# Modulation, scaling and first projections tile by tile at the start of a two-layer mixer backbone

## The chip, the cores and the metric

The kernel runs on one core of a Trainium2 chip. The metric is the device time of one execution in microseconds (us), the median over several runs.

## What is computed

A backbone of two layers over 512 tokens (256 of context and 256 latent) with 2048 features. Each layer normalises its input, shifts and scales it by a modulation vector that is computed from `c` (or from `c_ctx` for context tokens), projects it, sends the projections through four token mixers and merges their outputs. What the change touches is the beginning of the first layer:

```python
shift, scale, gate = jnp.split(jax.nn.silu(c) @ w_mod + b_mod, 3, axis=-1)
sh_c, sc_c, gt_c = jnp.split(jax.nn.silu(c_ctx) @ w_mod + b_mod, 3, axis=-1)
h = _rms(x, norm_g) * (1.0 + scale[:, None]) + shift[:, None]
hc = _rms(xc, norm_g) * (1.0 + sc_c) + sh_c
p = h @ w_in
pc = hc @ w_in
```

## The kernel before

The 2048 features lie in 16 feature tiles of 128 partitions, each with all 512 tokens along the free dimension. The sixteen tiles `x` are loaded, squared and summed (`sumsq`), and `rms_rows` makes one row of 512 scale factors of the sums, `rsb`: a matmul with a column of ones, a reciprocal square root on VectorE (`rq_y`), four transposes on TensorE (L305) and a copy on ScalarE (L525).

The modulation: `s32` holds silu of `c` and of `c_ctx`, a column pair per feature tile. `mod_unit` (L477) loads four pieces of `w_mod` of 128 x 512 (tag `mr`, 16 buffers, L487) and multiplies each with a pair of columns (L493). The four matmuls write to four groups of 32 rows of one bank, so that they can run beside each other. Eight units over two chunks of 512 columns (`shift` and `scale` of four feature tiles) accumulate in one bank. After the last unit ScalarE copies the bank to `ms` (L497), four matmuls with a selecting matrix (`sel`, L506) add up the row groups and turn the result, and VectorE adds the bias into `mod` (L509).

`build_h` (L528) makes of a tile `x` the modulated `h`: VectorE multiplies by `rsb`, ScalarE applies scale and shift for each half of the tokens, then rounds to the high part `Ra` (L542), and VectorE takes the low part `Rb`. `weights` (L370) loads a piece of `w_in` (`wr`, five buffers), ScalarE rounds it to `wh` (L375) and VectorE makes the rest `wl`. `mm3` (L379) multiplies with three matmuls: `wh` with `Ra`, `wh` with `Rb`, `wl` with `Ra`. `proj_part` (L385) does so for one name (a tile of 128 outputs) and one group of four feature tiles.

`run` (L1515) goes over the four groups `g` of four feature tiles. For each it builds `h` and then goes over eleven names: six that accumulate in banks of their own over all groups (`names`), and five whose parts are added up in memory (`more`). Beside the names of group `g` run the eight modulation units of group `g + 1`. Ahead of all stand the eight units of group 0:

```python
for _ in mods(0):
    pass
for g in range(4):
    s.build_h(xs, rsb, 4 * g, 4 * g + 4)
    md, done = mods(g + 1) if g < 3 else iter(()), 0
    for i, _ in enumerate(feats(g)):
        while done * nf < (i + 1) * 8:
            next(md, None)
            done += 1
```

All these loads are issued by SyncE in order. A scheduler below the program decides, within the dependencies, in which order each engine's instructions stand; the engines then take them in that order.

Of the kernel before, what the change touches and what calls it, by code (L numbers as in the profile page):

```python
# [13 lines left out]
ALU = mybir.AluOpType  # L14
# [32 lines left out]
_FI = {n: i for i, n in enumerate(_FN)}  # L47
# [6 lines left out]
_PO, _o = {}, 0  # L54
# [51 lines left out]
def pack(inp):  # L106
    f = lambda n: np.asarray(inp[n], dtype=np.float32)
    d = {}
    d["xT"] = np.ascontiguousarray(np.concatenate([f("ctx")[0], f("x")[0]], 0).T.reshape(KT, 128, T))
    d["cc"] = np.ascontiguousarray(np.stack([f("c")[0], f("c_ctx")], 1).reshape(KT, 128, 2).transpose(1, 0, 2))  # L110
    d["wmod"] = np.ascontiguousarray(f("w_mod").reshape(L, 16, 128, 12, 512).transpose(0, 3, 1, 2, 4))
    wi = f("w_in")
    win = np.zeros((L, _AB, 4, 128, 4, 128), np.float32)
    for n, i in _FI.items():
# [13 lines left out]
    par = np.zeros((L, 128, NPAR), np.float32)  # L128
# [20 lines left out]
    for n, a in (("al", f("d_alog")), ("dt", f("d_dtb"))):  # L149
        o, _ = _PO[n]  # L150
# [17 lines left out]
def wide(ap, n):  # L168

    return ap.rearrange("p (m o) -> p m o", o=1).to_broadcast([ap.shape[0], ap.shape[1], n])  # L170
# [17 lines left out]
class Kern:  # L188
# [193 lines left out]
        s.mm(ps, w[0], x[1], False, False)  # L382
        s.mm(ps, w[1], x[0], False, last)

    def proj_part(s, ps, l, name, t0, qt, alone=False):  # L385
        hi, lo = s.weights(s.i["win"][l, _FI[name], qt], [128, 4, 128])
        for k in range(4):
            kk = qt * 4 + k
            s.mm3(ps, (hi[:, k, :], lo[:, k, :]), (s.Hh[kk][:, t0:], s.Hl[kk][:, t0:]),
                  kk == 0 or alone and k == 0, kk == 15 or alone and k == 3)  # L390

    def proj_park(s, ps, l, name, t0):
# [84 lines left out]
    def mod_unit(s, l, chunks, u, pools, acc=False, bank=None):  # L477


        nc = s.nc  # L480
        i, nch = u // 4, len(chunks)
        first, last = u == 0, u == 4 * nch - 1
        raws = []
        for g in range(4):
            pool, tag = pools[g % len(pools)]
            raw = s.tl(pool, [128, 512], tag)
            nc.sync.dma_start(raw, s.i["wmod"][l, chunks[i], u % 4 * 4 + g])  # L487
            raws.append(raw)
        if first or not acc:
            s.mps = (bank or s.big)()  # L490
        ps = s.mps
        for g in range(4):
            s.mm(ps[32 * g:32 * g + 32, :], s.s32[:, u % 4 * 4 + g, 6 - 2 * i:38 - 2 * i], raws[g],  # L493
                 not acc or first, not acc or last)
        if last if acc else first:
            s.ms = s.tl(s.rp, [128, 512], "ms")
            nc.scalar.copy(s.ms, ps)  # L497
        elif not acc:
            s.tt(s.ms, s.ms, ps, ALU.add)
        if last:  # L500
            par, mod = s.lp[l]
            bo = _PO["bm"][0]
            w = 2 * nch
            p2 = (bank or s.big)()
            for f in range(4):
                s.mm(p2[:, w * f:w * f + w], s.ms[:, f * 128:(f + 1) * 128], s.c("sel", 0, w))  # L506
            pv = p2[:, 0:4 * w].rearrange("p (f i c) -> p i f c", f=4, c=2)
            for i, n in enumerate(chunks):
                s.tt(mod[:, n * 4:n * 4 + 4, :], pv[:, i], wide(par[:, bo + n * 4:bo + n * 4 + 4], 2), ALU.add)  # L509


    def sumsq(s, acc, x, first):
# [1002 lines left out]
    def run(s):  # L1515
        tc, nc = s.tc, s.nc
        with ExitStack() as ctx:
# [5 lines left out]
            with tc.tile_pool(name="x0", bufs=1) as xp:  # L1523
                acc = s.tl(xp, [128, T], "sqa")
                xs = []
# [5 lines left out]
                rsb = s.rms_rows(acc, xp)  # L1531
# [7 lines left out]
                def mods(g):  # L1539
                    for u in range(8):  # L1540
                        s.mod_unit(0, (g, 4 + g), u, [(xp, "mr")], True)
                        yield

                def feats(g):
                    for ps, name in zip(banks, names):
                        s.proj_part(ps, 0, name, 0, g)
                        if g == 3:
                            s.proj_park(ps, 0, name, 0)
                        yield
                    for name in more:  # L1550
                        ps = s.big()
                        s.proj_part(ps, 0, name, 0, g, True)
                        if g == 0:
                            part[name] = s.tl(xp, [128, T], "q" + name)
                            nc.scalar.copy(part[name], ps)
                        else:
                            s.tt(part[name], part[name], ps, ALU.add)
                        if g == 3:
                            nc.gpsimd.dma_start(s.pd[0][name], part[name])
                        yield  # L1560

                nf = len(names) + len(more)
                for _ in mods(0):
                    pass
                for g in range(4):
                    s.build_h(xs, rsb, 4 * g, 4 * g + 4)
                    md, done = mods(g + 1) if g < 3 else iter(()), 0
                    for i, _ in enumerate(feats(g)):
                        while done * nf < (i + 1) * 8:
                            next(md, None)  # L1570
                            done += 1
                s.done.update((0, name) for name in names + more)
                s.filling = False
            for l in range(L):
# [4 lines left out]
                with tc.tile_pool(name=f"xs{l}", bufs=1) as xp:  # L1579
                    xn, sqa = s.out_proj(xp)  # L1580
                    rsb = s.rms_rows(sqa, xp)
# [41 lines left out]
```

## Time and profile before

| what | us |
|---|---|
| median of 3 runs | 2807.53 |
| the runs | 2801.76, 2807.53, 2811.86 |
| the profiled execution's own time | 2812.09 |
| its span, first to last instruction | 2810.3 |
| mean granted TensorE clock | 0.976 |

The rows below come from the one profiled execution; times in them count from the start of its span. PE is TensorE's matmul, PEld its weight load, DVE VectorE, ACT ScalarE, SPq the instructions of SyncE that issue loads. A matmul of 32-bit floats without rounding has two records; x8 is four such matmuls. A name like `big<-mr,s` gives the written tile and those read; `big`, `mx`, `sc` and `acc` are PSUM banks.

### The profile page before, as it was taken

What the parts mean: (1) busy time and instruction counts of PE and PEld (TensorE: products, weight loads), DVE (VectorE), ACT (ScalarE), POOL (GpSimd) and SP (SyncE); (2) the same over time, 40 slices, a digit from 0 to 9 for tenths busy, and PEclk for the clock granted to TensorE, in tenths of its full rate; (3) what the DMA queues carried; (4) which work ended last, traced back from release to release, by engine and by line L of the source; (5) the groups of instructions that cost most, each with busy time, mean ns of one, the idle gap of its engine ahead of it and who ended that gap; (6) DMA issues with size and microseconds to landing.
All of it is one profiled execution on the core that took longest, in us unless ns stands there. A gap on an engine that the chain in (4) does not pass through costs nothing. (4 is left out here: it accounts for less than half of the span.)

```text
span 2810.3 us, 52526 instructions
## 1 busy us (share of the span) xinstructions
PE 2667.1 (95%) x19438; PEld 2035.5 (72%) x19438; DVE 1834.1 (65%) x5127; ACT 1277.1 (45%) x2737; POOL 180.0 (6%) x436
## 2 busy tenths in 40 slices
PE   7998999999999998999999999999999999999897
PEld 3666666677787777677787756776777877867897
DVE  4337776775486777866553354867866688678775
ACT  3334433443355555654442244444443356445553
POOL 0000000000000101000000000010100010100000
PEclk9999999999999998999999999999989999999999
DMA  9754243323432323325447886322323543423465
GB/s 340 266 188 139 78 134 107 121 87 97 122 123 68 101 92 99 97 61 161 151 115 261 272 279 204 112 80 63 110 67 94 161 139 100 128 88 93 144 190 160
DMA packets 210049, 385.80 MB, mean 137 GB/s; under 512 B 24640, under 2 KB 37824, under 8 KB 209792
## 3 DMA queue, kind: packets, MB, share of 16 engines
q1 hardware_dynamic: 199872, 351.23, 40.1%
q0 software_dynamic: 9920, 31.20, 3.0%
q8 instruction: 153, 2.51, 0.4%
q14 instruction: 104, 0.85, 0.1%
HBM read 346.95 MB, written 35.39 MB: 136 GB/s over the span
## 5 line engine op out<-in xcount | busy, mean ns | idle before, releaser
L283 PE MATMUL big<-Rb,wh 128*128 128x512 f32 (+1 forms) x3280 | 1097.3, 363 | 14.9 <-ACT Rb L1347 6.2
L375 ACT CAST wh<-wr 128x512 fp32r<-128x512 f32 x712 | 439.0, 620 | 801.3 <-PE big L283 572.3
L283 PE MATMUL big<-Ra,wh 128*128 128x512 f32 (+1 forms) x2128 | 771.9, 363 | 7.6 <-DVE po L315 3.4
L312 DVE TENSOR_TENSOR wl<-wr,wh 128x512 fp32r<-128x512 f32 x712 | 487.0, 687 | 335.3 <-ACT wh L375 299.6
L283 PEld LDWEIGHTS big<-Rb,wh 128*128 128x128 f32 x3280 | 610.8, 191 | 124.1 <-ACT raw L309 10.9
L283 PE MATMUL big<-Ra,wl 128*128 128x512 f32 (+1 forms) x1616 | 592.9, 367 | 5.2 <-DVE wl L312 5.1
L283 PEld LDWEIGHTS big<-Ra,wh 128*128 128x128 f32 x2128 | 405.9, 191 | 83.9 <-issue 9.9
L283 PE MATMUL big<-Rb,wl 128*128 128x512 f32 (+1 forms) x1088 | 379.7, 349 | 0.9 <-DVE wl L312 0.9
L283 PEld LDWEIGHTS big<-Ra,wl 128*128 128x128 f32 x1616 | 308.6, 191 | 51.1 <-DVE wl L312 6.5
L283 PEld LDWEIGHTS big<-Rb,wl 128*128 128x128 f32 x1088 | 207.4, 191 | 25.2 <-DVE wl L312 1.1
L312 DVE TENSOR_TENSOR iX<-iX,it 128x60 f32<-128x60 f32 (+24 forms) x744 | 182.7, 246 | 17.8
L312 DVE TENSOR_TENSOR it<-iB,iX 128x60 f32<-128x60 f32 (+24 forms) x744 | 173.7, 233 | 17.3
L315 DVE SCALAR_TENSOR_TENSOR po<-po,big 128x512 f32<-128x512 f32 (+1 forms) x128 | 70.4, 550 | 76.4 <-PE big L283 73.6
L283 PE MATMUL big<-Rb,wr 128*128 128x256 f32 (+1 forms) x448 | 112.4, 427 | 3.8 <-DVE Ra L315 2.4
L309 ACT ACTIVATE po<-big,gb 128x512 f32<-128x512 f32 (+1 forms) x128 | 74.0, 578 | 68.5 <-PE big L283 52.7
L283 PE MATMUL big<-mr,s 128*32 128x512 f32 x384 | 86.3, 619 | 17.5 <-DVE sqa L312 17.5
L283 PEld LDWEIGHTS big<-Rb,wr 128*128 128x128 f32 (+1 forms) x448 | 72.5, 183 | 25.0 <-issue 9.0
L315 DVE SCALAR_TENSOR_TENSOR cz<-raw,par,cz 128x508 f32<-128x508 f32 (+3 forms) x96 | 67.2, 700 | 6.0 <-ACT cz L309 5.4
L309 ACT ACTIVATE sw<-S,wc 128x64 f32<-128x64 f32 x96 | 33.4, 348 | 82.7 <-DVE S L315 75.3
L632 DVE TENSOR_REDUCE mx<-mx 128x1 f32<-128x512 f32 (+1 forms) x96 | 57.0, 598 | 20.8 <-PE mx L283 19.9
L283 PE MATMUL mx<-pT,avt 128*64 128x128 f32 x640 | 62.1, 292 | 1.5 <-ACT pT L658 1.3
L305 PE MATMUL mx<-cst,pt 128*128 128x128 f32 x320 | 52.9, 286 | 7.8 <-ACT pt L309 7.5
(373 smaller groups left out, 3760.2 us busy)
## 6 DMA issues: line engine op xcount, KB each, us to landing
wr<-in_win SPq DMA_DIRECT2D x440, 256.0 KB, 2.8
mr<-in_wmod SPq DMA_DIRECT2D x320, 256.0 KB, 4.9
wr<-in_wbr SPq DMA_DIRECT2D x128, 256.0 KB, 2.7
wr<-in_wout SPq DMA_DIRECT2D x128, 256.0 KB, 3.1
wr<-in_wmod SPq DMA_DIRECT2D x64, 256.0 KB, 3.8
wr<-in_gup SPq DMA_DIRECT2D x64, 256.0 KB, 2.7
x<-in_xT SPq DMA_DIRECT2D x16, 256.0 KB, 5.4
po<-y SPq DMA_DIRECT2D x16, 256.0 KB, 3.1
```

What stands on the lines that cost most here:

```text
L283: s.nc.tensor.matmul(o, l, r, start=start, stop=stop)
L305: s.nc.tensor.transpose(o, i, s.c("id"))
L309: s.nc.scalar.activation(o, i, f, bias=bias, scale=scale, **k)
L312: s.nc.vector.tensor_tensor(o, a, b, op)
L315: s.nc.vector.scalar_tensor_tensor(o, a, sc, b, op0, op1)
L375: s.nc.scalar.copy(hi, raw)
L632: nc.vector.tensor_reduce(mx[:, hc], ps[:, 0:nk], AX.X, ALU.max)
```

## The change

The first group of feature tiles is no longer modulated by eight units of whole chunks, but tile by tile. `mod_fine(k)` loads `shift` and `scale` of tile `k` alone, out of a copy of `w_mod` laid out for it (`wmf`, eight loads of 128 x 512), multiplies with 32 matmuls of 128 columns and one `sel` matmul, and adds the bias. Then tile `k` is built and the six `names` are projected for this tile alone, with weight pieces of 128 x 128. After the fourth tile the five `more` names follow with whole pieces, and beside these the eight units of group 1. Groups 1 to 3 are as before.

```diff
+    wm = f("w_mod")[0, :, 0:4096].reshape(4, 4, 128, 2, 16, 128)[:, :, :, :, 0:4]
+    d["wmf"] = np.ascontiguousarray(wm.transpose(4, 3, 0, 2, 1, 5))
...
-    def proj_part(s, ps, l, name, t0, qt, alone=False):
-        hi, lo = s.weights(s.i["win"][l, _FI[name], qt], [128, 4, 128])
-        for k in range(4):
+    def proj_part(s, ps, l, name, t0, qt, alone=False, ks=(0, 4)):
+        hi, lo = s.weights(s.i["win"][l, _FI[name], qt][:, ks[0]:ks[1], :], [128, ks[1] - ks[0], 128])
+        for k in range(*ks):
             kk = qt * 4 + k
-            s.mm3(ps, (hi[:, k, :], lo[:, k, :]), (s.Hh[kk][:, t0:], s.Hl[kk][:, t0:]),
+            s.mm3(ps, (hi[:, k - ks[0], :], lo[:, k - ks[0], :]), (s.Hh[kk][:, t0:], s.Hl[kk][:, t0:]),
                   kk == 0 or alone and k == 0, kk == 15 or alone and k == 3)
...
+    def mod_fine(s, k, pool):
+
+        ps, nc = s.big(), s.nc
+        for i in range(2):
+            raws = []
+            for g in range(4):
+                raw = s.tl(pool, [128, 512], "mr")
+                nc.sync.dma_start(raw, s.i["wmf"][k, i, g].rearrange("p a b -> p (a b)"))
+                raws.append(raw)
+            for c in range(4):
+                for g in range(4):
+                    s.mm(ps[32 * g:32 * g + 32, 0:128], s.s32[:, 4 * g + c, 6 - 2 * i:38 - 2 * i],
+                         raws[g][:, c * 128:c * 128 + 128], i == c == 0, i == 1 and c == 3)
+        ms = s.tl(s.rp, [128, 512], "ms")[:, 0:128]
+        nc.scalar.copy(ms, ps[:, 0:128])
+        p2 = s.big()
+        s.mm(p2[:, 0:4], ms, s.c("sel", 0, 4))
+        par, mod = s.lp[0]
+        bo = _PO["bm"][0]
+        for i in range(2):
+            s.tt(mod[:, 16 * i + k, :], p2[:, 2 * i:2 * i + 2], par[:, bo + 16 * i + k:bo + 16 * i + k + 1].to_broadcast([128, 2]),
+                 ALU.add)
...
-                def feats(g):
-                    for ps, name in zip(banks, names):
-                        s.proj_part(ps, 0, name, 0, g)
+                def feats(g, ks=(0, 4), only=None):
+                    for ps, name in zip(banks, names) if only != "more" else ():
+                        s.proj_part(ps, 0, name, 0, g, ks=ks)
...
-                for _ in mods(0):
-                    pass
-                for g in range(4):
-                    s.build_h(xs, rsb, 4 * g, 4 * g + 4)
-                    md, done = mods(g + 1) if g < 3 else iter(()), 0
-                    for i, _ in enumerate(feats(g)):
-                        while done * nf < (i + 1) * 8:
+                def beside(feats, n, md):
+                    done = 0
+                    for i, _ in enumerate(feats):
+                        while done * n < (i + 1) * 8:
                             next(md, None)
                             done += 1
+
+
+                s.mod_fine(0, xp)
+                for k in range(4):
+                    s.build_h(xs, rsb, k, k + 1)
+                    if k < 3:
+                        s.mod_fine(k + 1, xp)
+                    for _ in feats(0, (k, k + 1), "main"):
+                        pass
+                beside(feats(0, only="more"), len(more), mods(1))
+                for g in range(1, 4):
+                    s.build_h(xs, rsb, 4 * g, 4 * g + 4)
+                    beside(feats(g), len(names) + len(more), mods(g + 1) if g < 3 else iter(()))
```

SyncE's loads behind those for the first tile. In the kernel before, the last loads of group 0's modulation (`mr`) and the first of the weights (`wr`), with the semaphores that each waits for (DMAHW of earlier loads, PE and DVE of those engines):

```order
L487 DMA mr_467<-in_wmod 128x512 [waits DMAHW2_49,PE_49]
L487 DMA mr_469<-in_wmod 128x512 [waits DMAHW3_49,PE_49]
L372 DMA wr_518<-in_win 128x512 [waits DMAHW4_49]
L487 DMA mr_536<-in_wmod 128x512 [waits DMAHW5_49,PE_49]
L487 DMA mr_538<-in_wmod 128x512 [waits DMAHW6_49,PE_49]
```

With the change, from the last load for tile 1, over those for tile 2, to the weight piece of tile 1 that comes last:

```order
L521 DMA mr_474<-in_wmf 128x512 [waits DMAHW3_49]
L375 DMA wr_498<-in_win 128x128 [waits DMAHW4_49]
...
L375 DMA wr_534<-in_win 128x128 [waits DMAHW0_49]
L521 DMA mr_562<-in_wmf 128x512 [waits DMAHW1_49,PE_49]
L375 DMA wr_543<-in_win 128x128 [waits DMAHW4_49,DMAHW2_49,DVE_49]
L521 DMA mr_564<-in_wmf 128x512 [waits DMAHW3_49,PE_49]
...
L521 DMA mr_592<-in_wmf 128x512 [waits DMAHW1_49,PE_49]
L375 DMA wr_616<-in_win 128x128 [waits DMAHW2_49,DVE_49]
...
L521 DMA mr_680<-in_wmf 128x512 [waits DMAHW7_49,PE_49]
L375 DMA wr_661<-in_win 128x128 [waits DMAHW2_49,DMAHW0_49,DVE_49]
```

The sixth weight piece of each tile (`wr_543`, `wr_661`) now waits for VectorE, and seven loads of the tile after next stand behind it.

TensorE between two tiles, with the change: the last short matmuls of tile 2's modulation stand ahead of tile 1's first projection (`Ra_557`):

```order
L286 MATMUL acc_377<-Ra_439,wh_545 128x512
L286 MATMUL acc_377<-Rb_440,wh_545 128x512
L286 MATMUL big_561<-mr_564,s_4_254 32x128
L286 MATMUL acc_377<-Ra_439,wl_546 128x512
L286 MATMUL big_561<-mr_566,s_4_254 32x128
...
L286 MATMUL big_561<-mr_592,s_4_254 32x128
L286 MATMUL mx_372<-Ra_557,wh_618 128x512
L286 MATMUL mx_372<-Rb_558,wh_618 128x512
L286 MATMUL big_612<-cst_87,ms_610 128x4
```

In the kernel before there are no short matmuls; group 0's modulation is done there before the first projection.

TensorE at the end of the first group. Before, the `sel` matmuls (`big_809`) are followed by the last feature's twelve projections, and then by group 1's first (`Ra_842`):

```order
L283 MATMUL big_774<-Ra_514,wl_778 128x512
L283 MATMUL big_809<-cst_87,ms_807 128x4 x4
L283 MATMUL big_816<-Ra_490,wh_819 128x512
...
L283 MATMUL big_816<-Ra_514,wl_820 128x512
L283 MATMUL mx_372<-Ra_842,wh_872 128x512
```

With the change, the last unit's matmuls and `sel` (`big_1055`) come behind the last feature, and group 1's first projection (`Ra_1067`) behind four unit matmuls:

```order
L286 MATMUL big_1020<-Ra_793,wl_1024 128x512
L286 MATMUL big_880<-mr_1043,s_4_254 32x512
L286 MATMUL big_880<-mr_1045,s_4_254 32x512
L286 MATMUL big_880<-mr_1047,s_4_254 32x512
L286 MATMUL big_1055<-cst_87,ms_1053 128x4 x4
L286 MATMUL big_1121<-mr_1113,s_4_254 32x512
...
L286 MATMUL big_1121<-mr_1119,s_4_254 32x512
L286 MATMUL mx_372<-Ra_1067,wh_1097 128x512
```

VectorE ahead of the first freed weight buffer, with the change (`wl_501` is the split of `wr_498`, whose buffer `wr_543` takes):

```order
L318 SCALAR_TENSOR_TENSOR gs_433<-mod_259,par_257 128x2
L315 TENSOR_TENSOR Rb_440<-raw_435,Ra_439 128x512
L315 TENSOR_TENSOR raw_1079<-x_21_295,rsb_370 128x512
L315 TENSOR_TENSOR wl_501<-wr_498,wh_500 128x128
```

Two whole-tile operations stand between `gs` and that split.

## Rows read from the trace of the kernel before

**Rows 1.** The page's first part, busy us (share of the span) and instructions.
```profile
PE 2667.1 (95%) x19438; PEld 2035.5 (72%) x19438; DVE 1834.1 (65%) x5127; ACT 1277.1 (45%) x2737; POOL 180.0 (6%) x436
```

**Rows 2.** Busy time by stretch: length, engines, granted clock, DMA share, GB/s.
```profile
0.00:44.00 44.00, 23.75 (x91) 7.18 (x91) 18.40 (x43) 15.50 (x26) 0.21 (x4) 1.00 1.00 357
44.00:90.00 46.00, 45.58 (x198) 27.20 (x199) 14.32 (x24) 16.26 (x30) 0.00 (x0) 0.96 0.87 305
90.00:135.00 45.00, 45.00 (x207) 26.65 (x205) 16.22 (x29) 14.64 (x27) 0.00 (x0) 1.00 0.77 262
```

**Rows 3.** The timeline's weight loads 28 to 39 us, first and last of 16 (start, us).
```profile
28.26 0.14 PEld L283 LDWEIGHTS big<-mr,s 128*32 128x32 f32 x2 [0.54 <-DMA mr<-in_wmod]
...
38.43 0.14 PEld L283 LDWEIGHTS big<-mr,s 128*32 128x32 f32 x2 [0.55 <-DMA mr<-in_wmod]
```

**Rows 4.** The timeline from the row statistics to the first projection.
```profile
23.91 0.16 DVE L315 SCALAR_TENSOR_TENSOR rq_y<-rq_t,rq_y 128x4 f32<-128x4 f32 x1
25.17 0.65 PE L305 MATMUL mx<-cst,rq_y 128*128 128x128 f32 x4
25.86 0.58 ACT L525 COPY rsb<-mx 128x512 f32<-128x512 f32 x1 [8.44 <-PE mx L305]
...
38.43 1.04 PE L283 MATMUL big<-mr,s 128*32 128x512 f32 x2
39.51 0.58 ACT L497 COPY ms<-big 128x512 f32<-128x512 f32 x1 [13.07 <-PE big L283]
...
43.90 0.69 DVE L312 TENSOR_TENSOR Rb<-raw,Ra 128x512 fp32r<-128x512 f32 x1 [1.61 <-ACT Ra L542]
43.92 0.50 PE L283 MATMUL mx<-Ra,wh 128*128 128x512 f32 x1 [1.64 <-ACT Ra L542]
```

**Rows 5.** TensorE's timeline: the first unit matmul, then projections around a whole unit.
```profile
17.51 1.89 PE L283 MATMUL big<-mr,s 128*32 128x512 f32 x2 [17.51 <-DVE sqa L312]
...
62.51 0.39 PE L283 MATMUL mx<-Ra,wh 128*128 128x512 f32 x1
...
65.00 0.39 PE L283 MATMUL mx<-Ra,wl 128*128 128x512 f32 x1
65.32 1.06 PE L283 MATMUL big<-mr,s 128*32 128x512 f32 x8
66.32 0.50 PE L283 MATMUL acc<-Ra,wh 128*128 128x512 f32 x1
66.66 0.39 PE L283 MATMUL acc<-Rb,wh 128*128 128x512 f32 x1
```

**Rows 6.** Small operations: TensorE's timeline, then groups by line with mean ns.
```profile
622.72 0.28 PE L283 MATMUL sc<-vt,tok 64*64 64x64 f32 x4
622.84 0.28 PE L283 MATMUL acc<-AT,vt 64*64 64x64 f32 x4
...
L309 ACT ACTIVATE vn<-sc 128x128 f32<-128x128 f32 x24 | 6.5, 272 | 4.2 <-PE sc L283 4.2
L312 DVE TENSOR_TENSOR mx<-mx,cm 128x128 f32<-128x128 f32 x32 | 9.5, 297 | 16.9 <-PE mx L283 16.7
```

**Rows 7.** Issues of `mr` loads to 60 us: min, median, max ns; us to landing.
```profile
L487 SPq DMA_DIRECT2D mr<-in_wmod x57: 327/328/385, 12.0 to 59.7; - x57
...
DMA to landing us min/median/max: 3.0/5.4/6.9
```

**Rows 8.** TensorE's timeline at the end of the first group.
```profile
85.79 0.95 PE L283 MATMUL big<-cst,ms 128*128 128x4 f32 x8
...
90.00 0.39 PE L283 MATMUL mx<-Ra,wh 128*128 128x512 f32 x1
```

**Rows 9.** Busy time by stretch, as in rows 2, around two falls of the clock.
```profile
45.80:49.20 3.40, 3.40 (x7) 1.01 (x6) 3.25 (x6) 3.13 (x7) 0.00 (x0) 0.52 1.05 383
219.60:221.70 2.10, 0.14 (x2) 0.02 (x1) 2.04 (x5) 1.98 (x4) 0.00 (x0) 1.00 0.00 0
222.90:226.80 3.90, 3.90 (x14) 1.38 (x12) 2.68 (x9) 0.60 (x1) 0.10 (x1) 0.56 0.00 0
```

More of the change, by code (lines that the diff above doesn't have):

```diff
@@ L1549, in feats @@
                         yield
-                    for name in more:
+                    for name in more if only != "main" else ():
                         ps = s.big()
@@ L1560, in feats @@
                         yield
-                nf = len(names) + len(more)
-                for _ in mods(0):
-                    pass
-                for g in range(4):
-                    s.build_h(xs, rsb, 4 * g, 4 * g + 4)
-                    md, done = mods(g + 1) if g < 3 else iter(()), 0
-                    for i, _ in enumerate(feats(g)):
-                        while done * nf < (i + 1) * 8:
+                def beside(feats, n, md):
+                    done = 0
+                    for i, _ in enumerate(feats):
+                        while done * n < (i + 1) * 8:
                             next(md, None)
                             done += 1
+                s.mod_fine(0, xp)
[9 more added lines that the diff above has]
+                    beside(feats(g), len(names) + len(more), mods(g + 1) if g < 3 else iter(()))
                 s.done.update((0, name) for name in names + more)
```

## The prediction

> **What bounds the kernel now.** I read the page's busy shares first: TensorE (PE) is busy for 95% of the span, no other engine for more than 65% [rows 1]. So a gain must come from PE's idle stretches, or from work taken off PE. Then the table by stage, with bounds at the first projection matmul of each group of four feature tiles: 0 to 44 us is the only stretch in which PE is far from full (23.75 us of 44), and the first two groups after it take 46 and 45 us with PE full [rows 2]; so do the other two. After 179 us the order of the instructions is the same in both kernels, so what is won or lost by then is carried to the end. The question is only when each group's first projection starts.
>
> Why does PE wait until 43.92 us? In the waits of its weight loads, PE stands behind the 32 loads of modulation weights (`mr`): from 28.26 to 38.43 us 16 weight-load rows follow each other, each ended by a landing, so one 256 KB load lands every 10.17/15 = 0.68 us [rows 3], with the DMA engines full (share 1.00, [rows 2]). Then comes a chain: `ms` on ScalarE, four `sel` matmuls, the adds into `mod`, `gs`, two activations, the cast to `Ra`, first projection: 39.46 (38.43 + 1.04) to 43.92, 4.5 us [rows 4].
>
> **The change part by part.** The sum is made against the profiled execution, 2812.09 us with a span of 2810.3, which is 0.16% above the median of 2807.53; I carry the difference over.
>
> *Earlier start.* Tile 0 now needs 8 loads, not 32, so the data would be there 24 x 0.68 = 16 us earlier, at about 22 us. Something else is then late: the row statistics. Their last `rq_y` ends at 24.07, their transposes ran only at 25.17, queued on PE behind full-length `mr` matmuls, and `rsb` is ready at 26.44 [rows 4]. With short ones ahead the transposes start about 1 us earlier, at 24.1. Behind them stand 27 or so of tile 0's 32 short matmuls. PE starts slowly: a matmul of 512 columns took 1.89 us at 17.51, where four beside each other took 1.06 at 65.32 [rows 5]. In that ratio a short round of four, 0.25 us later on (below), takes 0.45 here: seven rounds, 3.2 us, to 27.9. The chain of 4.5 us shrinks: `ms` is 128 wide (0.3 for 0.58), one `sel` matmul (0.3) stands for four (0.95, [rows 8]): 3.5 us. First projection at about 31.5, **12.4 us earlier**. Bounds: 30.0 if the short matmuls already run at the higher level, 32.5 if the chain keeps all but 0.1 us of its 4.5.
>
> *Short matmuls.* Per tile there are 32 matmuls of 128 columns, in rounds of four beside each other. No row shows this shape. The lower bound is the pace of short matmuls: four records of 64x64 in 0.12 us [rows 6], so eight in 0.24. The upper bound is the full-length round, 1.0 us [rows 5]. With a quarter of the columns it is nearest the lower: 0.25. Tile 1's run while PE waits for the first chain. Tiles 2 and 3 have 16 rounds: 4.0 us. Three small `sel` matmuls at 0.3: 0.9. Switching between the shapes costs: a full-length round between projections takes 65.23 to 66.32 and delays the next matmul by 0.11, so 1.2 us for 1.0 [rows 5]; four lone short matmuls stand among projections (0.45 each, with both switches) and two blocks are switched to: 2.3. Together **+7.2 us** on PE. They were not there before: the long units beside them stay 32 matmuls, in about 12 rounds in either order, and cost the same.
>
> *The load queue.* SyncE issues in order. As the order shows, `wr_543` waits for VectorE to free a weight buffer (the pool has five), and the seven remaining modulation loads of tile 2 stand behind it. VectorE frees it after `Rb_440`, `raw_1079` (0.69 each, [rows 4]) and the split `wl_501` (0.3, [rows 6]): 31.1 + 1.7 = 32.8. From there a turn is: issue 0.33, first landing 3.0 after its issue (the shortest row, [rows 7]), six more loads at 0.68, the first weight piece 0.33, its cast and split 0.6 [rows 6]: 8.3 us. PE has 18 projections of 0.228 (4.1 us, [rows 5]) and about 2.5 of short work in such a turn, and since the short matmuls stand ahead of the next tile's projections, it waits. Tile 1's projections start at 32.8 + 7.4 + 0.5 = 40.7, tile 2's at 49.0, and tiles 2 and 3 are done at 57.5. PE's own work would have ended at 31.5 + 16.5 + 7.2 = 55.2: **+2.3 us**.
>
> A weight piece is 64 KB in rows of 512 B. The trace has no such load. By bytes it takes 0.17 us of the DMA engines, by its 128 rows, as many as a 256 KB load has, up to 0.68. I take the 0.33 us that SyncE needs to issue it [rows 7], and keep both ends. The Trainium skill ("DMA: Bandwidth & Descriptors", Specifications) says 512 B is the least transfer that still runs at line rate; by that it would be 0.17 us, and the sum would not move, since the issue is slower; no run here shows it.
>
> *End of the first group.* Before, the last `sel` matmuls (85.79) were followed by twelve projections of the last feature, to 90.00, and these hid the chain to the next group's first `Ra` [rows 8]. In the changed order the last unit's matmuls come after the last feature, and behind the `sel` matmuls stand only four unit matmuls (1.2 us) before `Ra_1067`. So the chain of 4.5 us lies open, less those 1.2 us, which belong to the next group, and less the 1.4 us that `sel` already cost between 85.79 and the twelve projections (90.00 less 12 x 0.228 is 87.2): **+1.9 us**. What is late next is ScalarE, which makes one feature tile in 1.7 us where PE has 0.7 us of projections for each name: the second group then starts as slowly as the first did before, 46 us instead of 45 [rows 2]: **+0.9 us**.
>
> The loads of the second group's modulation units (32 x 0.68 us, plus four weight loads) start at about 52, land by 80 and are needed until 85: hidden. ScalarE's six casts of 0.3 instead of one of 0.62 per name are hidden beside 4.1 us of projections; without that cover they would cost 0.3 us a tile.
>
> Sum: -12.4 + 7.2 + 2.3 + 1.9 + 0.9 = -0.1 us. **Forecast: no change, 2807 us** (0.3% is 8.4 us, about what a measurement of this kernel can tell from no change). With the best ends (start at 30.0, no waits, no slow second group) it is -4.8 us, with pieces at 0.68 us +3.6.
>
> **The rivals.** *The lead is kept.* PE has projections waiting whenever the queue is late, and the short matmuls fall into waits that cost nothing: -12.4 + 1.9 + 0.9 = -9.6 us, 2798. For it: PE is full in every stage after the first and DMA is at 0.87 of its time or less [rows 2], so a lead is not eaten later. Against it: PE takes instructions in order, and the order has the short ones ahead of the projections. Chance 0.11.
>
> *PE falls to its lower clock level after each new gap.* The granted clock was 0.52 from 45.8 to 49.2, after the wait for the first `Ra`, and 0.56 from 222.9 to 226.8, after 2.1 us with 0.14 of work [rows 9]; those are stretches at the level of 1.2 GHz instead of 2.4. Some 3.9 us at half the pace cost 1.95. The change makes three thin stretches, two turns of the queue and the open chain: 5.8 us, if nothing hides it. Add pieces that cost 0.68: fourteen loads in a turn make 9.5 us, not 8.3, three times: 3.6. Then -0.1 + 5.8 + 3.6 = +9.3 us, 2817, slower. It decides from about +8.4 us: when all three gaps are paid and a piece costs over 0.6 us. Against it: in two of the three the queue, not PE, sets the pace. The Trainium skill ("TensorE: Matmul & The Clock Gate", HAM oscillation) warns of just this: waits on loads between bursts of matmuls send PE back to half rate, and the way up is paid again each time. The trace agrees with it at 222.9 [rows 9]. A short round at 1.0 us instead of 0.25 would come out there too (+12). Chance 0.14.
>
> That the change does not do what it says can be left out: the order shows the tile-by-tile start.
>
> **How the numbers follow.** No change within 8.4 us has 0.75, faster 0.11, slower 0.14. The range takes in the slower case and stops short of the faster one's 2798: 2799 to 2817.
>
> **What would show it.** Right: the first projection at 30 to 32.5 us; the second, third and fourth tile's at 40.7, 49 and about 53; SyncE waiting on VectorE at `wr` loads of 64 KB; the second group's first projection near 90, with PE idle 2 to 4 us ahead of it. Wrong: PE full from 31.5 on and the second group at 80 to 82 (the lead is kept), or a granted clock near 0.5 in several stretches from 36 to 60 us and the second group after 95.

## The result: slower by 0.6%, then by 0.3%

| | us |
|---|---|
| changed kernel, median of 7 runs | 2825.23 (2815.77 to 2832.11) |
| kernel before, beside it, median of 7 | 2807.53 (2801.76 to 2811.91) |
| ratio, 95% interval | 1.0059 (1.0039 to 1.0079) |
| second measurement (12 and 35 runs, below) | 2821.78 and 2813.03, ratio 1.0028 (1.0013 to 1.0043) |
| profiled execution of the change: its time, its span | 2822.74, 2820.9 |

The forecast was 2807 us and no change. The profile after shows where the time went. Its busy time by stretch, columns as in [rows 2]; the last two stretches overlap the others:

```profile
0.00:32.50 32.50, 9.71 (x143) 7.55 (x143) 17.81 (x42) 14.41 (x26) 0.21 (x4) 1.00 0.84 293
32.50:64.00 31.50, 28.33 (x206) 19.57 (x206) 11.56 (x41) 11.55 (x36) 0.00 (x0) 0.95 0.68 216
64.00:96.00 32.00, 29.43 (x142) 13.92 (x141) 4.64 (x10) 8.68 (x17) 0.00 (x0) 1.00 1.03 373
28.00:36.00 8.00, 6.10 (x89) 4.58 (x83) 4.73 (x16) 4.37 (x13) 0.00 (x0) 1.00 0.17 52
24.00:64.00 40.00, 34.98 (x330) 24.95 (x330) 15.98 (x52) 14.37 (x42) 0.00 (x0) 0.96 0.66 210
```

The last row has its counterpart in the kernel before:

```profile
24.00:64.00 40.00, 37.69 (x145) 15.75 (x144) 14.90 (x26) 11.95 (x22) 0.00 (x0) 0.96 1.02 370
```

PE did begin earlier, and in those 40 us it was busy nearly as long. But the DMA engines, full before (370 GB/s), moved only 210: 52 GB/s from 28 to 36 us. Then, from 64 to 96 us, they run full to catch up. PE's timeline shows what that means; the bracket at a row's end is the idle time before it and what ended it:

```profile
32.49 0.50 PE L286 MATMUL mx<-Ra,wh 128*128 128x512 f32 x1 [1.14 <-ACT wh L378]
...
41.07 0.41 PE L286 MATMUL big<-mr,s 128*32 128x128 f32 x2 [0.69 <-DMA mr<-in_wmf]
...
43.41 0.50 PE L286 MATMUL mx<-Ra,wh 128*128 128x512 f32 x1
...
52.12 0.41 PE L286 MATMUL big<-mr,s 128*32 128x128 f32 x2 [0.97 <-DMA mr<-in_wmf]
...
54.38 0.80 PE L286 MATMUL mx<-Ra,wh 128*128 128x512 f32 x1
...
64.08 0.50 PE L286 MATMUL big<-Ra,wh 128*128 128x512 f32 x1
...
92.23 1.05 PE L286 MATMUL big<-cst,ms 128*128 128x4 f32 x8 [0.75 <-ACT ms L500]
93.21 1.06 PE L286 MATMUL big<-mr,s 128*32 128x512 f32 x8
95.94 0.50 PE L286 MATMUL mx<-Ra,wh 128*128 128x512 f32 x1 [1.66 <-ACT Ra L568]
```

The tiles' first projections stand at 32.49, 43.41 and 54.38 us, 11 us apart, and before the second and the third PE waits for modulation loads. The five late names start at 64.08, and the second group at 95.94 instead of 90.00. Why the loads are late stands on SyncE's queue, first its issues, then its waits from 20 to 64 us (total, times, longest):

```profile
26.60 0.33 SPq L521 DMA_DIRECT2D mr<-in_wmf  x1
33.91 0.33 SPq L375 DMA_DIRECT2D wr<-in_win  x1
34.33 3.27 SPq L521 DMA_DIRECT2D mr<-in_wmf  x7
37.69 2.63 SPq L375 DMA_DIRECT2D wr<-in_win  x5
41.09 0.33 SPq L521 DMA_DIRECT2D mr<-in_wmf  x1
43.34 0.33 SPq L375 DMA_DIRECT2D wr<-in_win  x1
43.79 4.97 SPq L521 DMA_DIRECT2D mr<-in_wmf  x7
...
51.22 0.38 SPq L490 DMA_DIRECT2D mr<-in_wmod  x1
53.71 4.16 SPq L375 DMA_DIRECT2D wr<-in_win  x5
```

```profile
SPq L375 <- DVE mod L315: 6.0, 1, 6.0
SPq L375 <- DVE wl L315: 5.0, 8, 1.2
```

From 26.93 to 33.91 us SyncE issues nothing: the sixth weight piece waits for VectorE, and seven modulation loads stand behind it. (The row names `mod` as VectorE's result; what ends just before 33.91 is the split `wl`.) Shorter stops follow from 41.42 to 43.34 and from 51.60 to 53.71.

How much of this reaches the end? From the fourth group on the order of the work is the same in all kernels here, so I compare one row of VectorE, the fourth group's `gs`. Before, then after:

```profile
176.73 0.17 DVE L315 SCALAR_TENSOR_TENSOR gs<-mod,par 128x8 f32<-128x8 f32 x1
```

```profile
184.06 0.17 DVE L318 SCALAR_TENSOR_TENSOR gs<-mod,par 128x8 f32<-128x8 f32 x1
```

It is 7.3 us late: 5.9 at the second group's start, and 1.4 in the second group, which takes 46.6 us instead of 45.2. From this row to the end the two executions took 2633.6 us before and 2636.8 after. The median says 16.6 (0.0059 x 2807.5), with an interval of 11 to 22; the remaining 9 us are taken up in the second measurement.

### The profile page after: what moved, and what is told of

Its sections match the earlier page's. It is cut to its first block, busy times and chain, and to the rows that moved or that the text cites. A ratio compares the mean times of both kernels' runs of the same rounds, so it can differ in the third digit from the quotient of the medians.

```text
span 2820.9 us, 53024 instructions
## 1 busy us (share of the span) xinstructions
PE 2669.2 (95%) x19630; PEld 2046.5 (73%) x19630; DVE 1836.8 (65%) x5154; ACT 1279.8 (45%) x2758; POOL 180.1 (6%) x436
## 5 line engine op out<-in xcount | busy, mean ns | idle before, releaser
L378 ACT CAST wh<-wr 128x512 fp32r<-128x512 f32 (+1 forms) x730 | 441.4, 609 | 810.6 <-PE big L286 587.4
L315 DVE TENSOR_TENSOR wl<-wr,wh 128x512 fp32r<-128x512 f32 (+1 forms) x730 | 489.4, 674 | 350.9 <-ACT wh L378 329.4
L286 PEld LDWEIGHTS big<-Rb,wh 128*128 128x128 f32 x3280 | 612.4, 192 | 124.0 <-ACT raw L312 10.9
L286 PE MATMUL big<-mr,s 128*32 128x512 f32 (+1 forms) x576 | 82.2, 481 | 20.7 <-DMA mr<-in_wmf 20.6
```

The costliest lines, as they stand in the source:

```text
L286: s.nc.tensor.matmul(o, l, r, start=start, stop=stop)
L315: s.nc.vector.tensor_tensor(o, a, b, op)
L378: s.nc.scalar.copy(hi, raw)
```

## The experiments

Theory Q: the load queue. SyncE's order lets modulation loads stand behind waiting weight pieces; the DMA engines idle, and that idle time pushes the second group. Theory C: the open chain at the end of the first group. Theory P: PE itself, by short matmuls or by falls of its clock. The table has the first projection, that of the second group, the fourth group's `gs` against the kernel before (176.73), all from one profile each, and the ratio of medians with its interval.

| run | first | second group | `gs` | ratio |
|---|---|---|---|---|
| own buffers for pieces | 33.49 | 86.06 | -1.3 | 0.9980 (0.9964 to 0.9996) |
| chain hidden | 32.75 | 97.31 | +3.6 | 1.0022 (1.0004 to 1.0040) |
| both | 31.89 | 88.98 | -4.7 | 0.9977 (0.9957 to 0.9997) |
| fine modulation, whole projections | 45.99 | 92.51 | +2.3 | 0.9984 (0.9967 to 1.0002) |
| the change again | 32.10 | 94.75 | +6.2 | 1.0028 (1.0013 to 1.0043) |
| whole weights | 33.13 | 94.75 | +6.1 | 1.0024 (1.0008 to 1.0039) |
| whole weights, chain hidden | 32.75 | 96.26 | +2.6 | 1.0002 (0.9985 to 1.0020) |
| before, 11 loads added | 52.33 | 98.35 | +8.4 | 1.0036 (1.0018 to 1.0055) |
| pieces on GpSimd | 33.85 | 90.66 | +3.2 | 1.0017 (1.0001 to 1.0033) |
| own buffers, GpSimd, chain hidden | 35.82 | 95.22 | +1.5 | 1.0019 (1.0004 to 1.0034) |
| both, again | 32.44 | 89.43 | -4.3 | 0.9983 (0.9965 to 1.0000) |
| both, units spread | 33.20 | 85.66 | -3.3 | 0.9991 (0.9972 to 1.0009) |

Where the chain is hidden, the late projections and some units have moved ahead of the second group's first projection or behind it, so that column is compared within one order only; `gs` is comparable everywhere.

### Buffers of their own

```diff
-        raw = s.tl(s.wp, shape, "wr")
+        raw = s.fp.tile(shape, F32, tag="wf", name=s.nm("wf"), bufs=18) if shape[1] == 1 else s.tl(s.wp, shape, "wr")
```

> The change with 18 buffers of their own for the 128 x 128 weight pieces, so that SyncE no longer stands behind VectorE there; arithmetic as in the change. Theory Q (the load queue): the DMA engines were idle from about 28 to 35 us and again near 42, 48 and 54 us, and the 32 modulation loads of the second group, 0.68 us each, came late by that; with full engines from 28 us on all loads for the second group have landed by about 75 us, PE sets the pace, first projection still at 32.5, second group's first projection at 86 to 88 instead of 95.94, total some 8 us below the change (about 2815 to 2818 in the median where the change has 2825). Theory C (the open chain at the end of the first group): the second group moves by under 2 us. Theory P (PE's own work, short matmuls and clock): PE has no more waits but the phases take as long, second group still at 93 or later.

SyncE, PE and the DMA engines of this run:

```profile
27.51 3.87 SPq L521 DMA_DIRECT2D mr<-in_wmf  x8
...
36.36 4.19 SPq L521 DMA_DIRECT2D mr<-in_wmf  x8
40.61 7.95 SPq L375 DMA_DIRECT2D wf<-in_win  x12
```

```profile
33.49 0.80 PE L286 MATMUL mx<-Ra,wh 128*128 128x512 f32 x1
...
55.80 0.39 PE L286 MATMUL big<-Ra,wh 128*128 128x512 f32 x1
...
82.35 1.05 PE L286 MATMUL big<-cst,ms 128*128 128x4 f32 x8 [0.74 <-ACT ms L500]
86.06 0.79 PE L286 MATMUL mx<-Ra,wh 128*128 128x512 f32 x1 [1.66 <-ACT Ra L568]
```

```profile
24.00:64.00 40.00, 38.66 (x370) 29.04 (x371) 18.04 (x56) 15.18 (x44) 0.00 (x0) 1.00 0.91 302
46.00:48.00 2.00, 1.81 (x35) 1.37 (x31) 0.39 (x2) 0.90 (x5) 0.00 (x0) 1.00 0.31 90
```

Only the buffers differ in the program, and the tiles take 22.3 us (33.49 to 55.80) instead of 31.6; the second group starts 9.9 us earlier, as theory Q expected. One thing more moves with the buffers: the scheduler now sets a tile's short matmuls in one block, where the change has two lone ones among the projections of each of the first two tiles. At the prediction's price of 0.45 us each these four are 1.8 of the 9.3 us, so the queue has some 7.5. Of the 22.3 us, 72 projections of 0.228 are 16.4; 5.9 are left for the short and selecting matmuls and the switches, and PE is busy for 22.1. So theory P has a share too, one that buffers do not win back, and theory C keeps its 3.7 us (82.35 to 86.06). The second row of the last fence prices a piece: with only pieces under way the engines moved 90 GB/s at a share of 0.31, 290 at full share, so 0.23 us for 64 KB; SyncE issued twelve in 7.95 us, 0.66 each, waits for earlier landings included.

### The chain hidden, alone and with the buffers

```diff
-                beside(feats(0, only="more"), len(more), mods(1))
+                beside(feats(0, only="more"), len(more) - 1, mods(1))
```

> The change with the eight units of the second group placed beside the first four of the five late features, so that the last feature's twelve projections follow the selecting matmuls; nothing else. Theory C: those twelve (2.7 us) cover the chain to the second group's first projection: 93 to 93.5 instead of 95.94, and no fall of the granted clock near 98, which is worth another 1 us; total 3 to 4 us below the change. Theory Q: the last unit waits for its loads at about 89 us whatever stands behind it, so 2 to 2.7 us at most, and only at this place. Theory P: under 1 us.

> Own buffers for the weight pieces and the units beside four of the five late features. If queue and chain are two separate losses, they add up: second group's first projection at 83 to 85 us, 5 to 7 us ahead of the kernel before (90.00), total 2800 to 2803. If the loads bind the whole first stage (16 + 32 + 32 loads and the weights, 84 us of full DMA engines), the second group cannot start before about 84 to 87. If PE's own work binds (theory P): 92 or later, total near 2815.

The first projections of the second group, alone and with own buffers:

```profile
97.31 0.50 PE L286 MATMUL mx<-Ra,wh 128*128 128x512 f32 x1 [1.62 <-ACT wh L378]
```

```profile
79.52 1.05 PE L286 MATMUL big<-cst,ms 128*128 128x4 f32 x8 [0.74 <-ACT ms L500]
...
88.98 0.50 PE L286 MATMUL mx<-Ra,wh 128*128 128x512 f32 x1 [1.33 <-ACT wh L378]
```

I expected the second group at 93 to 93.5 and at 83 to 85. Both missed: the chain is covered, but the cast of the second group's first weights is now late. The weights themselves are not. With own buffers SyncE issues their first piece at 73.28, and it lands 5.4 us later; ScalarE casts it at 88.32. ScalarE's order, where this cast stands behind the copy of the last feature's bank, and the landing of that piece:

```profile
85.83 0.59 ACT L1582 COPY qBk<-big 128x512 f32<-128x512 f32 x1 [1.15 <-PE big L286]
...
88.32 0.60 ACT L378 CAST wh<-wr 128x512 fp32r<-128x512 f32 x1
```

```profile
DMA to landing us min/median/max: 5.4/5.4/5.4
```

The copy waits for PE to finish the last feature, and from there to the cast ScalarE has no gap. It is the same with the chain hidden alone (issued at 82.46, landed 5.4 us later, cast at 96.65). By the `gs` hiding the chain is still worth 2.5 to 3.7 us (7.3 or 6.2 to 3.6), and 3.4 with own buffers (-1.3 to -4.7): the two losses add up. With both the median is 0.23% below that of the kernel before (0.9977).

### Fine modulation without tile-by-tile projections

```diff
+                for k in range(4):
+                    s.mod_fine(k, xp)
                 for g in range(4):
                     s.build_h(xs, rsb, 4 * g, 4 * g + 4)
```

> Modulation of the first four tiles tile by tile with short matmuls, but shift and scale, weights and projections by whole groups as in the kernel before. The scale of all four tiles waits for the last tile's modulation, so the first projection is at 42.5 to 43.9 us, the second group's at 88.5 to 90.5, total within 2 us of the kernel before: short matmuls that run in waits cost nothing (theories Q and C). Theory P: the short matmuls or the gaps between them cost wherever they stand: second group at 93 or later, total 4 us or more above the kernel before.

The first projection is 2.1 us later than I allowed at most, the second group's 2.0, and `gs` is 2.3 late. The trace shows a wait of the queue here too: there are 16 `mr` buffers, and SyncE waits 3.4 us, to 26.31, for PE to free the first of them, so the last of the 32 loads is issued at 35.97 us (33.0 in the kernel before) and the fourth tile's `sel` stands at 42.84. The median agrees with the kernel before within its interval. Against theory P: 128 short matmuls in waits cost 2.3 us at most, not 6.

### The change again, and a mere shift

The second kernel is the kernel before with loads that nobody reads ahead of the first group's modulation:

```diff
+                for i in range(11):
+                    raw = s.tl(xp, [128, 512], "mr")
+                    nc.sync.dma_start(raw, s.i["wmod"][0, 8, i])
                 for _ in mods(0):
                     pass
```

> The changed kernel once more, as it is. The first stage (second group's first projection at 95.94 us against 90.00) accounts for 6 to 7 us; the median of the change was 17 us above that of the kernel before, from seven runs each. If the rest is scatter that comes with the number of low-clock stretches later in the program, the ratio comes out near 1.0025 (some 7 us) with the first stage as before; if the change does something systematic to the later part, again 1.005 to 1.007.

> The kernel before with eleven more loads of 256 KB ahead of the first modulation loads; nothing reads them. If each load in that queue is worth its 0.68 us up to the second group, the first projection moves from 43.92 to 51.4 and the second group's from 90.00 to 97.5, and the total by 7 to 8 us (ratio 1.0025 to 1.003): a mere shift of the first stage by what the change loses there. If a shift sets off more low-clock stretches later, as the change's median would suggest: 14 us or more (ratio 1.005).

The change comes out at 1.0028, 7.9 us (interval 3.7 to 12.1), with a `gs` 6.2 us late: the first stage is enough to explain it. The eleven loads move the first projection by 8.4 us, 0.76 each, and `gs` by the same 8.4; the ratio is 10 us, with an interval of 5 to 15. A shift of the first stage reaches the end about one for one, and nothing shows that it costs more later. That the first measurement's other 9 us were scatter is likely, but no run shows it by itself: the kernel before had a median of 2807.5 in 7 runs there, and of 2812 to 2815 in each later series. From `gs` to the end, in the same order, the profiled executions of all the kernels here took 2626 to 2639 us.

### Whole weights

The six names' weights come as six loads of 256 KB and stay; each tile casts its part.

```diff
+                for i, name in enumerate(names):
+                    raw = s.tl(s.wp, [128, 4, 128], "wr") if i < 2 else xp.tile([128, 4, 128], F32, tag="wf", name=s.nm("wf"), bufs=4)
+                    nc.sync.dma_start(raw, s.i["win"][0, _FI[name], 0])
+                    s.whole[name] = raw
```

> The change with the six names' weights loaded as whole pieces of 256 KB (six loads instead of 24), kept, and cast tile by tile; so no wait of SyncE for VectorE and no small loads. With own buffers and small pieces the queue issued one 64 KB piece per 0.6 to 0.75 us and moved 90 to 260 GB/s there where whole loads move 387. Theory Q, with the small pieces as its second half: the loads for the second group end 6 to 9 us earlier than with own buffers and small pieces (its last modulation load was issued at 82.5), PE sets the pace, second group's first projection at 82 to 85 us (own buffers: 86.06). If small pieces cost nothing (0.22 us each on the DMA engines by the packets): 86 again. First projection at 32 to 33 in either case.

> Whole weights as in the run before, and the second group's units beside four of the five late features. With own buffers this order gained nothing in the first projection of the second group, since its first weights stood behind the modulation loads (88.98, waiting for the cast of the weights). If the loads now end early enough, the chain is hidden and the weights are there: second group's first projection at 81 to 84 us without a wait for the weights' cast, and a total of 6 to 9 us below the kernel before. If PE or the loads still bind: 86 or later and not over 4 us below.

The first is at 94.75, as late as the change; of the second the last branch came out (96.26, no gain). The reason that its expectation gives for 88.98 does not hold: that cast was late by ScalarE's order, not by the loads. SyncE's waits (34 to 76 us) and the DMA engines in the first of the two runs:

```profile
SPq L492 <- PE big L286: 16.2, 5, 9.6
SPq L523 <- PE big L286: 8.6, 3, 7.8
```

```profile
36.00:44.00 8.00, 7.58 (x91) 4.47 (x93) 1.97 (x8) 1.76 (x6) 0.00 (x0) 0.96 0.30 93
64.00:72.00 8.00, 8.00 (x43) 5.24 (x43) 2.61 (x6) 2.84 (x6) 0.00 (x0) 1.00 0.05 16
```

The wait for VectorE is gone, and one for PE has taken its place. With 16 `mr` buffers, tile 3's loads need those of tile 1, and PE now has tile 1's short matmuls spread among tile 0's projections: SyncE issues nothing from 33.41 to 41.32. Later the second group's first loads fill the buffers early, while PE takes them only beside the late names, and SyncE stops from 61.14 to 70.68. The DMA engines are nearly empty from 64 to 72 us, and the gain is gone. That agrees with theory Q in its general form (idle DMA engines set the second group's start). What the small pieces cost it does not tell, since another stop came in their place.

### Small pieces out of SyncE's queue

```diff
-        s.nc.sync.dma_start(raw, src)
+        (s.nc.gpsimd if shape[1] == 1 else s.nc.sync).dma_start(raw, src)
```

> The change with the 24 small weight pieces issued by GpSimd, not by SyncE; still in the five shared buffers. If the loss is that modulation loads stand behind a waiting weight piece in SyncE's order (theory Q), taking the pieces out of that queue is enough, without more buffers: the DMA engines stay busy from 28 to 36 us, tile 1's, 2's and 3's first projections follow each other by 6 to 8 us instead of 10.9, and the second group's first projection is at 86 to 89, total 7 to 10 us below the change (ratio to the kernel before 0.998 to 1.000). If the buffers themselves are what is short (the pieces come too late for TensorE), the tiles stay 9 us or more apart and the second group at 92 or later.

> Own buffers for the pieces, issued by GpSimd, and the second group's units beside four of the five late features. SyncE then issues whole loads only: with 0.6 to 0.75 us per small piece gone from its order, the loads for the second group end 6 us or more earlier than with own buffers alone (last modulation load issued at 82.5 there). Theory Q: second group's first projection at 82 to 85 us, second group's weights in time, total 6 to 9 us below the kernel before (ratio 0.997 to 0.998). If TensorE's own work binds by then: 84 to 86 and a ratio of 0.998 or above. The pieces are now issued early, among the loads of the input tiles, and may put the row statistics off by up to 3 us; the first projection would then be at 35.

With the five shared buffers, the second group starts at 90.66: 4 to 5 us better than the change, between the two forecasts (86 to 89, and 92 or later). The DMA engines are busy from 28 to 36 us as theory Q has it (share 0.94 instead of 0.17), and the tiles stand 8.6, 8.2 and 7.9 us apart. But the whole pieces of the late names still share the five buffers, and there SyncE stops from 47.11 to 56.56, modulation loads behind it. By `gs` (6.2 to 7.3 late, then 3.2, and 1.3 ahead with own buffers) the pieces' place in the queue is about one half of the loss, and the shared buffers are the other.

With own buffers and the hidden chain the pieces on GpSimd are a loss: `gs` +1.5, where with SyncE it was -4.7. Of these some 6 us the later first projection (35.82 for 31.89 and 32.44) has 3.4 to 3.9, where I allowed 3. The waits of this run, from 20 to 90 us:

```profile
SPq L490 <- PE big L286: 18.6, 9, 9.6
SPq L521 <- PE big L286: 8.0, 6, 4.0
```

Again the 16 buffers: SyncE, now free of pieces, runs ahead of PE and stops there. It looks as if the pieces in SyncE's order, by spacing the modulation loads, kept them near the pace at which PE frees their buffers; that was not tried by itself. The cast of the second group's first weights is late here too, as above.

### The best version again, and with units spread

Four of the second group's units move up among the projections of the third and fourth tile:

```diff
+                md = mods(1)
...
-                    for _ in feats(0, (k, k + 1), "main"):
-                        pass
+                    for i, _ in enumerate(feats(0, (k, k + 1), "main")):
+                        if k > 1 and i in (2, 5):
+                            next(md)
+                beside(feats(0, only="more"), 2 * len(more) - 2, md)
```

> Own buffers and hidden chain (as in the run before of that kind) once more, beside a version that spreads the units. First stage some 5 us ahead of the kernel before by 179 us, ratio again near 0.998 if that is real; 1.000 if the first reading was scatter.

> As the run beside it, and four of the second group's eight units move up among the projections of the third and fourth tile, one beside each of four late features. The modulation loads are then taken out of their 16 buffers earlier, and more of the work on TensorE is full-length matmuls in the stretch where the short ones wait. If loads or their buffers still bind (theory Q), the DMA engines' idle time after 24 us shrinks below 2.6 us and the second group's first projection comes 1 to 3 us earlier than 86 to 89; ratio 0.996 to 0.998. If TensorE's own work binds (theory P: the short matmuls' 6 us are a price that no order takes away, and what the lead of 11.4 leaves is 5.5), nothing moves: 0.9975 to 0.999.

Own buffers with the hidden chain repeat: `gs` -4.3, ratio 0.9983. By `gs` that is the best version here; by the medians it is some 5 to 6 us below the kernel before (0.9977 and 0.9983), with upper ends of 0.9997 and 1.0000, at the edge of no difference. Spreading the units gains nothing by `gs` (-3.3), though the cast of the second group's first weights now comes early (80.67) and its first projection at 85.66; so nothing shows that the late cast of the other orders costs anything by `gs`. What is left would be mostly PE's: a lead of 11 to 12 us less 5.9 for short matmuls is 5 to 6, and the `gs` has 4.3 to 4.7 of it. That is a sum and not shown by a run, and with both changes PE still idles for 2.6 of the 26 us from 64 to 90.

## Why the prediction was wrong

By its own steps:

- *Earlier start*, forecast 31.5 us: measured 32.49, a lead of 11.4 instead of 12.4. Right within its bounds (30.0 to 32.5). The short matmuls end at 28.5 instead of 27.9; the chain behind them takes 4.0 us for 3.5, in part since ScalarE casts `wh` only behind `Ra`, and the first projection waits for `wh`.
- *Short matmuls*, forecast 0.25 us a round and +7.2 in all: the profile has 64 records, eight rounds, in 1.96 us, 0.245 each, and the run with own buffers leaves 5.9, without the four lone matmuls that the forecast had at 1.8. Right within 0.5.

```profile
29.39 1.96 PE L286 MATMUL big<-mr,s 128*32 128x128 f32 x64
```

- *The load queue* **failed, in its size.** The place and the mechanism were named (the sixth weight piece behind VectorE, seven loads behind it); a turn was put at 8.3 us, and the term at +2.3. Measured: SyncE resumes at 33.91, 43.34 and 53.71, turns of 9.4 and 10.4, and tiles 1 and 2 start 10.9 and 11.0 us after the one ahead. By the prediction's own reckoning the term is 64.08 less 32.49, 16.5 and 7.2: 7.9 us. The part of the turn that was wrong is "six more loads at 0.68". The first load behind each stop landed as forecast, 2.8 and 3.0 us after its issue (forecast 3.0). The last of the seven landed at 42.4 and 52.8, so the six came 0.87 and 1.0 us apart. The seven loads of the first turn, the landing times of those of the second, and PE's last waits for both:

```profile
L521 SPq DMA_DIRECT2D mr<-in_wmf x7: 382/382/422, 34.3 to 37.2; - x7
...
DMA to landing us min/median/max: 2.8/4.1/5.2
```

```profile
DMA to landing us min/median/max: 3.0/3.9/4.5
```

```profile
42.42 1.06 PE L286 MATMUL big<-mr,s 128*32 128x128 f32 x26 [0.30 <-DMA mr<-in_wmf]
...
52.81 1.64 PE L286 MATMUL big<-mr,s 128*32 128x128 f32 x26 [0.29 <-DMA mr<-in_wmf]
```

The step counts one small piece, at the end of the turn. SyncE issues five behind the seven loads, and the DMA engines move them while the last of the seven still land. Their packets from 41.0 to 42.4 us:

```profile
DMA packets 734, 0.44 MB, mean 314 GB/s; under 512 B 85, under 2 KB 664, under 8 KB 734
```

Of these, 579 (664 less 85) have the size of the pieces' rows, 512 B and more; five pieces have 640 such rows. At 0.23 us each, five pieces make 1.1 us, as much as the first turn's six landings were late; no run separates it. In the second turn SyncE issues more slowly too, seven loads in 4.97 us for 3.27, with waits for earlier loads and for PE. The turn closes through the queue itself: the pieces land behind the seven loads, only then are they cast and split, and only then is the buffer free that SyncE waits for.

```profile
42.69 0.30 ACT L378 CAST wh<-wr 128x128 fp32r<-128x128 f32 x1 [6.01 <-DMA wr<-in_win]
```

With the median of 5.4 us from issue to landing [rows 7] in place of 3.0 a turn would have come out at 10.7, near what was measured, but by the wrong step.

- *Loads of the second group hidden*: the step gave their start as 52 us. Three of them were issued before 59, and the engines were full up to 96. The run with own buffers shows that this was the same loss, not a second one: late names and units took 26.6 us there (55.80 to 82.35) and 28.2 here (64.08 to 92.23), so only 1.6 us more of it lie behind 64.08.
- *End of the first group*, forecast +1.9 and +0.9: the chain from the end of the last unit matmul to `Ra` took 4.5 us (91.48 to 95.94), as forecast, 3.7 of it from the `sel` matmuls on. Hiding it was worth 2.5 to 3.7, by `gs`; the slow start of the second group cost 1.4 for 0.9. Nearly right.

By the forecast's sum the second group stood at 89.0; it came at 95.94, 6.9 us later. Of these, 1.0 is the first projection, 5.6 the queue (7.9 for 2.3) and 0.3 the rest. The second measurement's 7.9 us would even lie within the 8.4 that the forecast called no change. That is no credit to the sum, which had -0.1 us where `gs` has 6.2 to 7.3. (Its end of +3.6 for pieces at 0.68 us is 3.5 with the -0.1 counted in, which changes nothing.)

Of the rivals, *the lead is kept* was wrong as stated, but the run with both mended comes, by `gs`, within some 5 us of it. *PE falls to its lower clock level after each new gap* gave 2817, nearest to what was measured, by the wrong mechanism; only its turn of 9.5 us is near the measured ones, and that by a piece at 0.68 us, where 0.23 was measured. The granted clock in the first profile, and in the second profile of the same kernel over the same stretch:

```profile
52.80:57.00 4.20, 4.19 (x34) 3.40 (x35) 1.28 (x7) 1.76 (x7) 0.00 (x0) 0.59 0.28 95
```

```profile
52.80:57.00 4.20, 4.20 (x29) 3.31 (x21) 1.96 (x9) 3.26 (x11) 0.00 (x0) 1.00 0.39 124
```

Once PE fell to the level of 1.2 GHz there, once it did not. Ahead of it PE was busy for 7.24 and 7.39 of the 8.80 us from 44.0. From the third tile's first projection to the late names it took 9.70 us with the fall (54.38 to 64.08) and 10.15 without (53.15 to 63.30), of which 1.4 were a wait for weights. So the fall cost some 0.9 us by these two executions, in one of them, and the rival's 5.8 us for three such gaps are not there. The fall after the open chain (0.66 from 96 to 101 in both) stands for the one at 45.8 in the kernel before [rows 9].

The Trainium skill ("TensorE: Matmul & The Clock Gate", HAM oscillation) tells of waits on loads between bursts of matmuls that send PE back to half rate. The trace agrees with it in one of the two executions, and in the other such waits brought no fall.

The Trainium skill ("DMA: Bandwidth & Descriptors", Specifications) has 512 B as the least transfer at line rate, by which a piece would take an estimated 0.17 us. The row at 46 us gives 0.23, and the measurement decides.

## What to carry to other kernels

A load queue that is taken in order couples everything that stands in it: before putting small loads with few buffers between large ones, follow each wait one turn round (load, matmul, chain, cast, buffer, load), with all that the DMA engines move in that turn and all that the issuing engine waits for. Here the first landing came as forecast, and those behind it 0.87 to 1.0 us apart instead of 0.68. If the stage's DMA engines were nearly full before, every microsecond in which they idle is a candidate for the end time, so read the DMA share of the stage first, and then which buffer it is that stops the queue; taking one wait away can move the stop to the next scarce buffer, as with whole weights and with GpSimd here. When a first matmul waits for a cast, look when the data had landed before blaming the load; here it had, and it was the casting engine's order that was late. Of a lead won at the start, what PE pays for the finer work (5.9 of 11.4 us here) is gone whatever the queue does.

## What the runs showed that I had not expected

The same kernel's executions differ, and with them PE's mean granted clock. The version with both changes, profiled in two series, took 2808.7 us at a mean granted clock of 0.974 and 2799.9 us at 0.979. 8.8 us lie between two executions of one program that were less than 0.5 us apart at `gs`. So a median of seven runs can be off by several us, as that of the kernel before seems to have been in the first measurement. Why the low stretches later in the program vary from one execution to the next stays open; no run here was made for it.
